# Hybrid encoder, border of mixer and feed-forward: the transposes of x's second half follow the gate's first two products in the program

## The chip, the cores and the metric

The kernel runs on one core of one Trainium2 chip. The metric is the device time of one execution in microseconds. Before the change three runs took 617.32, 617.40 and 617.11 us, a median of 617.32.

A core has five engines that work beside each other, each through its own list of instructions in order: TensorE (PE in the profile, with its weight loads as PEld), VectorE (DVE), ScalarE (ACT), GpSimd (POOL) and SyncE (SP, which issues DMAs here).

## The reference, cut to what matters

An encoder of two layers works on x of 256 tokens by 1024 columns. In each layer a mixer (three kinds of attention heads side by side) adds its output to x, and a feed-forward with a gated, convolved hidden width of 2816 does the same:

```python
for l in range(DEPTH):                       # DEPTH = 2
    x = mixer_sublayer(x, ...)               # ends in: return x + mix @ w_out_l
    x = channel_sublayer(x, ...)

def channel_sublayer(x, n2, w_gu, cw, cb, w_dn):
    h = rms_norm(x, n2)
    g, u = jnp.split(h @ w_gu, 2, axis=-1)
    g = depthwise_conv_centred(g, cw, cb)
    return x + (jax.nn.gelu(g, approximate=False) * u) @ w_dn
```

## The kernel before, in words

**Numbers as pairs.** Every large product is made of float32 values that are split into a high part and a low part (high rounded, low the rest). ACT makes a high part, DVE the low part from it. For weights these are `wp_hi` and `wp_lo`, made from `wp_raw`, the form that DMA brings in; `split` (line 607) does it in quarters of 512 columns for a unit of the feed-forward. For x they are the two halves of the tile `act_hT`.

**The border.** x lies in SBUF as `xs` (in the profile `const_x`), 128 tokens on the partitions, two token tiles t = 0 and 1, 1024 columns. The mixer ends with output projections, six pieces in `OUT_ORDER` (line 72). The last two, group 2 into columns 0 to 511 and into columns 512 to 1023, stand at lines 1246 and 1249. Each piece makes 6 matmuls for each token tile into a PSUM tile of `psa`, and then DVE adds the result to that half of `xs`.

The feed-forward needs x with its columns on the partitions. `split_T` (line 649) does this for one half of x: four column blocks k, two token tiles each, so 8 transposes on PE into two PSUM tiles of the pool `psw`; then for each k ACT writes the high part with the norm's gain, and DVE the low part. Line 1248 does the first half (k = 0 to 3), between the two projections. `mean_squares` (line 673, called at 1251) lets ACT sum the squares of x for the norm's scale, in four pieces, and POOL finishes it. The scale itself, `r2`, is applied later to the products, so transposes needn't wait for it.

**Gate and up.** The feed-forward goes through 11 steps of 256 hidden columns in the order of `FFN` (line 74): G0, U0, G1, D0, U1 and so on (G gate, U up, D down). A gate or up product is `half_up` (line 1259). It has two output tiles j = 0, 1 in `psw`, and for each of them eight column blocks k. What is called a product in this text is one `part(j, k)`, two matmuls: high weights with both parts of x (512 columns) and low weights with the high part (256 columns). G0 is called with `first=True`, and has the second half's `split_T` inside (line 1274): the first half's eight products (k = 0 to 3 for j = 0 and 1), then the transposes, then k = 4 to 7, then `row_scale`, two transposes of `r2`. A down step adds to four tiles in `psa` that stay until the end.

**What orders the work.** The code doesn't issue instructions as it is read. It writes them into a `Plan`. `order` (line 303) then chooses, one by one, among all the operations whose predecessors are placed, the one that can start first by the planner's own costs and handover times; among those with equal starts the one of the lower rank goes first (lines 366 and 367):

```python
                    if at is not None and (best is None or (at, o.rank) < best[:2]):
                        best = (at, o.rank, i)
```

The start `at` is the latest of the operands' readiness, the engine's freedom, and the freedom of a buffer for a tile that is used for the first time. The rank is the place in the program plus a shift (line 260). Casts and low halves of weights have a shift of 50 (`SPLIT_LATER`, line 56), so they stand behind what comes up to 50 places later, when both could start. Buffers of one pool are given out in the order of the tiles' first use in the program (`t.turn`, line 308; line 326 holds a tile back until its turn). `psw` has four. The planned order of each engine is then what the chip does; each engine waits on semaphores for what it needs.

Weights are loaded ahead: `unit` (line 625) is called by each product and brings the split of the next unit and the loads of those behind it. So U0's weights are cast and split while G0 is computed, and G0's while the last projection is. There are four buffers of `wp_raw` and two each of `wp_hi` and `wp_lo`.

The profile gives line 413 for every instruction, the one in `emit` that hands a planned operation to its engine. So instructions are told apart by engine, operation and tiles.

Of the kernel before, what the change touches and what calls it, by code (L numbers as in the profile page):

```python
# [455 lines left out]
def encoder_kernel(  # L456
# [168 lines left out]
    def unit():  # L625

        i = taken[0]
        taken[0] += 1
        with nc.later(SPLIT_LATER):
            while len(raws) < min(i + AHEAD + RAWS - PARTS, len(views)):  # L630
                load(len(raws))
            while len(parts) < min(i + AHEAD, len(views)):
                split(len(parts))
        return parts[i]
# [14 lines left out]
    def split_T(srcs, hi, lo, k0, g, name):  # L649


        n = g.shape[1]
        for b in range(0, n, 2):
            m = min(2, n - b)
            ps = psw.tile([P, 2, S], F32, tag="w", name=f"pt_{name}_{b}")
            for i in range(m):
                k = b + i
                for t in range(NT):
                    nc.tensor.transpose(
                        ps[:, i, t * P : (t + 1) * P], srcs[t][:, k * P : (k + 1) * P], ident  # L660
                    )
            for i in range(m):
                k = b + i
                h, o = hi[:, k0 + k], lo[:, k0 + k]
                nc.scalar.activation(h, ps[:, i], AF.Copy, scale=g[:, k : k + 1])
                nc.vector.scalar_tensor_tensor(
                    o, ps[:, i], g[:, k : k + 1], h.bitcast(F32), ALU.mult, ALU.subtract
                )

    def halves(h):  # L670
        return [xs[:, t, h * 512 : (h + 1) * 512] for t in range(NT)]
# [144 lines left out]
    for l in range(DEPTH):  # L816
# [442 lines left out]
        def half_up(name, first=False):  # L1259

            wh, wl = unit()
            ps = [psw.tile([P, 2, S], F32, tag="w", name=f"{name}{j}") for j in range(2)]

            def part(j, k):
                js = slice(j * P, (j + 1) * P)
                nc.tensor.matmul(ps[j], wh[:, k, js], h2[:, k], start=k == 0, stop=False)
                nc.tensor.matmul(ps[j][:, 0], wl[:, k, js], h2_hi[:, k], start=False, stop=k == KD - 1)

            if first:
                for k in range(4):  # L1270
                    part(0, k)
                for k in range(4):
                    part(1, k)
                split_T(halves(1), h2_hi, h2_lo, 4, gains[:, 2, l, 4:8], f"n2{l}1")
                for k in range(4, KD):
                    part(0, k)
                for k in range(4, KD):
                    part(1, k)
                row_scale()
                return ps  # L1280
            for j in range(2):
                for k in range(KD):
                    part(j, k)
            return ps

        def row_scale():

            for t in range(NT):
                nc.tensor.transpose(
                    rps[:, t * P : (t + 1) * P], r2[:, t : t + 1].to_broadcast([P, P]), ident  # L1290
                )
            nc.vector.tensor_copy(rb, rps[:, :S])
# [11 lines left out]
        def gate(s):  # L1304
            nm = f"{l}_{s}"
            Gs = joined(half_up(f"G{nm}", s == 0), f"Gs{nm}")
            nc.vector.tensor_tensor(Gs, Gs, rb.unsqueeze(1).to_broadcast([P, 2, S]), op=ALU.mult)
            A = act.tile([P, 2, S], F32, tag="s2k", name=f"A{nm}", bufs=NS2K)
            for j in range(2):
                f = 2 * s + j  # L1310
                col = lambda i: cw[:, 22 * i + f : 22 * i + f + 1]
                nc.scalar.activation(A[:, j], Gs[:, j], AF.Identity, bias=col(3), scale=col(1))
                nc.vector.scalar_tensor_tensor(
                    A[:, j, 1:S], Gs[:, j, 0 : S - 1], col(0), A[:, j, 1:S], ALU.mult, ALU.add
                )
                nc.vector.scalar_tensor_tensor(
                    A[:, j, 0 : S - 1], Gs[:, j, 1:S], col(2), A[:, j, 0 : S - 1], ALU.mult, ALU.add
                )
            B = act.tile([P, 2, S], F32, tag="s2k", name=f"B{nm}", bufs=NS2K)
            nc.scalar.activation(B, A, AF.Gelu)  # L1320
            made[s] = B

        def up(s):
            nm = f"{l}_{s}"
            C = joined(half_up(f"U{nm}"), f"C{nm}")
            nc.vector.tensor_tensor(C, made[s], C, op=ALU.mult)
            ch = act.tile([P, 2, S], F32R, tag="ch", name=f"ch{nm}", bufs=2)
            cl = act.tile([P, 2, S], F32R, tag="cl", name=f"cl{nm}", bufs=2)
            nc.scalar.copy(ch, C)
            nc.vector.tensor_tensor(cl, C, ch.bitcast(F32), op=ALU.subtract)  # L1330
            ready[s] = (ch, cl)
# [114 lines left out]
```

## Time and profile before

| | |
|---|---|
| median of 3 runs | 617.32 us (617.11 to 617.40) |
| profiled execution, span from the first to the last instruction | 615.5 us |
| instructions | 9869 |
| busy PE / DVE / ACT / POOL | 98% / 79% / 70% / 14% |
| HBM traffic | 196 GB/s over the span |
| granted clock of TensorE | 1.000 |

The profiled execution's own time is known by its span alone: 615.5 us, 1.8 us under the median of the runs, which also holds what lies before the first and behind the last instruction.

Views of the trace give a start, a duration, the engine, the operation, and the tiles as output<-inputs. A row ending in x4 stands for four instructions in a row, with the time from the first's start to the last's end; since instructions of one engine overlap a little in the pipeline, rows of single instructions overlap too. In brackets stands how long the engine was idle before the row, and what ended the wait. Layer 0's border lies at about 114 to 133 us, layer 1's at 414 to 433 us.

### The profile page before, as it was taken

The numbers are of one execution on the slowest core, as the hardware profiler recorded it, in microseconds if no ns is written. First come the engines' busy times: TensorE is split into PE (matmuls) and PEld (weight loads), VectorE is DVE, ScalarE is ACT, GpSimd is POOL, SyncE is SP. The second block draws the span as 40 slices with busy tenths as digits, with TensorE's granted clock in tenths as the row PEclk, the third lists the DMA queues.
The fourth block names the chain that finished last, engine by engine and source line by source line (L and its number), as shares of the span: only waits on it lengthen the run. The fifth ranks groups of instructions, "written<-read, shape, count | busy, mean of one in ns | idle before, by whom it ended". The sixth has DMA issues, their size and how long they took to land.

```text
span 615.5 us, 9869 instructions
## 1 busy us (share of the span) xinstructions
PE 604.9 (98%) x3484; PEld 523.7 (85%) x3484; DVE 486.9 (79%) x1000; ACT 428.3 (70%) x1064; POOL 84.0 (14%) x136
## 2 busy tenths in 40 slices
PE   8999999999999999999999999998999999999997
PEld 7998878888888888888899988887888888888885
DVE  4888989888778988878867797867877777777774
ACT  6888989686566677666588898866755656556651
POOL 2741230212400000000032213333000000000000
PEclk9999999999999999999999999999999999999999
DMA  8894313656596999988445644554565566555501
GB/s 287 275 291 143 102 35 104 208 192 195 164 252 235 364 353 325 309 278 269 154 150 173 222 137 171 205 175 135 179 231 171 176 204 205 166 180 201 185 21 68
DMA packets 85073, 121.44 MB, mean 197 GB/s; under 512 B 9864, under 2 KB 69608, under 8 KB 85024
## 3 DMA queue, kind: packets, MB, share of 16 engines
q1 hardware_dynamic: 82752, 112.17, 55.6%
q0 software_dynamic: 1728, 8.39, 4.0%
q8 instruction: 27, 0.44, 0.3%
q10 hardware_dynamic: 544, 0.26, 0.2%
q14 instruction: 22, 0.18, 0.1%
HBM read 110.93 MB, written 9.88 MB: 196 GB/s over the span
## 4 chain that ended last, share of the span: by engine, by line
PE 92%; DVE 3%; ACT 2%; issue 1%; DMA 1%; POOL 0%; SPq 0%; DVEq 0%; ACTq 0%
PE psw_w L413 49%; PE psa_a L413 43%; DVE const_x L413 1%; ACT act_s2k L413 1%; DVE wp_lo L413 1%; DMA wp_raw<-in_w_in_dram 1%; DVE act_hT L413 1%; ACT act_hT L413 1%; ACT wp_hi L413 1%; POOL small_rstd L413 0%; ACT act_mixT_hi L413 0%; POOL small_ms L413 0%; SPq L413 0%; DVE act_mixT_lo L413 0%; DVE small_ss L413 0%
## 5 line engine op out<-in xcount | busy, mean ns | idle before, releaser
L413 DVE TENSOR_TENSOR wp_lo<-wp_raw,wp_hi 128x512 fp32r<-128x512 f32 (+2 forms) x332 | 232.3, 731 | 42.9 <-ACT wp_hi L413 41.4
L413 PE MATMUL psw_w<-act_hT,wp_hi 128*128 128x512 f32 x704 | 247.8, 397 | 2.1 <-DVE act_hT L413 2.1
L413 ACT CAST wp_hi<-wp_raw 128x512 fp32r<-128x512 f32 (+2 forms) x332 | 203.1, 662 | 26.1 <-PE psw_w L413 15.3
L413 PE MATMUL psw_w<-act_hT,wp_lo 128*128 128x256 f32 x704 | 196.1, 279 | 0.1
L413 PEld LDWEIGHTS psw_w<-act_hT,wp_hi 128*128 128x128 f32 x704 | 131.9, 188 | 34.1 <-DVE act_hT L413 3.0
L413 PEld LDWEIGHTS psw_w<-act_hT,wp_lo 128*128 128x128 f32 x704 | 132.6, 188 | 1.5 <-DVE wp_lo L413 0.4
L413 PE MATMUL psa_a<-wp_hi,act_hT 128*128 128x384 f32 (+2 forms) x448 | 112.8, 332 | 0.7 <-ACT act_hT L413 0.5
L413 ACT COPY act_s2k<-psw_w 128x256 f32<-128x256 f32 x88 | 32.4, 373 | 76.3 <-PE psw_w L413 76.3
L413 PEld LDWEIGHTS psa_a<-wp_hi,act_hT 128*128 128x128 f32 x448 | 77.9, 189 | 3.8 <-ACT act_hT L413 1.0
L413 PE MATMUL psa_a<-wp_lo,act_hT 128*128 128x384 f32 (+2 forms) x224 | 74.7, 334 | 0.0
L413 PE MATMUL psa_a<-wp_lo,act_ch 128*128 128x512 f32 x176 | 69.5, 395 | 0.0
L413 PE MATMUL psa_a<-wp_hi,act_ch 128*128 128x512 f32 x176 | 69.4, 394 | 0.0
L413 PE MATMUL psa_a<-wp_hi,act_cl 128*128 128x512 f32 x176 | 65.8, 394 | 0.0
L413 DVE TENSOR_TENSOR act_s2k<-psw_w,act_s2k 128x256 f32<-128x256 f32 x88 | 36.8, 422 | 31.1 <-ACT act_s2k L413 30.7
L413 PEld LDWEIGHTS psa_a<-wp_lo,act_hT 128*128 128x128 f32 x224 | 42.3, 189 | 2.0 <-DVE wp_lo L413 1.0
L413 PEld LDWEIGHTS psa_a<-wp_hi,act_ch 128*128 128x128 f32 x176 | 33.1, 188 | 7.9
L413 PEld LDWEIGHTS psa_a<-wp_hi,act_cl 128*128 128x128 f32 x176 | 33.2, 188 | 7.8
L413 PEld LDWEIGHTS psa_a<-wp_lo,act_ch 128*128 128x128 f32 x176 | 33.1, 188 | 6.9
L413 DVE SCALAR_TENSOR_TENSOR act_s2k<-act_s2k,act_cw,act_s2k 128x255 f32<-128x255 f32 x88 | 36.9, 478 | 1.5 <-ACT act_s2k L413 1.3
L413 POOL TENSOR_TENSOR small_rstd<-small_ms,const_mh 128x6 f32<-128x6 f32 (+2 forms) x26 | 31.6, 1216 | 2.2
L413 ACT ACTIVATE act_s2k<-act_s2k,act_cw 128x256 f32<-128x256 f32 x44 | 24.1, 595 | 9.8 <-DVE act_s2k L413 9.4
L413 PE MATMUL psw_w<-act_ch,const_v 128*128 128x256 f32 x128 | 28.6, 286 | 1.1 <-ACT act_s2k L413 1.1
(112 smaller groups left out, 779.3 us busy)
## 6 DMA issues: line engine op xcount, KB each, us to landing
wp_raw<-in_w_gate_up_dram SPq DMA_DIRECT2D x44, 1024.0 KB, 5.1
wp_raw<-in_w_down_dram SPq DMA_DIRECT2D x22, 1024.0 KB, 4.8
wp_raw<-in_w_in_dram SPq DMA_DIRECT2D x14, 768.0 KB, 5.3
wp_raw<-in_w_in_dram SPq DMA_DIRECT2D x8, 1024.0 KB, 6.3
wp_raw<-in_w_out_dram SPq DMA_DIRECT2D x8, 768.0 KB, 6.4
dram_khi<-act_mixT_hi SPq DMA_DIRECT2D x4, 768.0 KB, 4.3
dram_klo<-act_mixT_lo SPq DMA_DIRECT2D x4, 768.0 KB, 5.6
wp_lo<-dram_klo POOLq DMA_DIRECT2D x4, 768.0 KB, 4.8
```

What stands on the lines that cost most here:

```text
L413: getattr(o.engine.real, o.method)(*map(real, o.args), **{k: real(v) for k, v in o.kw.items()})
```

## The change

In `half_up`, for G0 alone, the call that transposes and splits x's second half moves up in the program: it follows the product of k = 0 for the two output tiles, and the other six products of the first half follow it. The products of k = 1 to 3 keep their order. No instruction is added, removed or altered, in either layer; what the planner is given is another sequence, and so other ranks.

```diff
             if first:
-                for k in range(4):
-                    part(0, k)
-                for k in range(4):
-                    part(1, k)
+                for j in range(2):
+                    part(j, 0)
                 split_T(halves(1), h2_hi, h2_lo, 4, gains[:, 2, l, 4:8], f"n2{l}1")
+                for j in range(2):
+                    for k in range(1, 4):
+                        part(j, k)
                 for k in range(4, KD):
                     part(0, k)
                 for k in range(4, KD):
```

## The prediction

> **What bounds the kernel now.** I read the page first, then the busy time by stretches, then who PE waits for, then the order of time at the two borders of mixer and feed-forward.
>
> ```profile
> span 615.5 us, 9869 instructions
> ## 1 busy us (share of the span) xinstructions
> PE 604.9 (98%) x3484; PEld 523.7 (85%) x3484; DVE 486.9 (79%) x1000; ACT 428.3 (70%) x1064; POOL 84.0 (14%) x136
> ```
>
> PE is busy 98% of the span, so a change is worth what it takes out of PE's own waits, 615.5 - 604.9 = 10.6 us at first sight. In the next view each stretch has its length, then busy time of PE, PEld, DVE, ACT and POOL, then the granted clock.
>
> ```profile
> 114.00:133.00 19.00, 17.86 (x100) 14.58 (x99) 16.32 (x33) 14.69 (x34) 4.31 (x6) 1.00 0.60 197
> 133.00:304.00 171.00, 171.00 (x901) 145.67 (x901) 141.56 (x239) 111.92 (x203) 9.52 (x18) 1.00 0.80 265
> 304.00:311.50 7.50, 7.50 (x43) 6.35 (x42) 5.19 (x9) 4.57 (x14) 0.00 (x0) 1.00 0.56 165
> 311.50:414.00 102.50, 101.91 (x691) 93.17 (x690) 79.82 (x223) 85.23 (x288) 29.25 (x43) 1.00 0.53 177
> 414.00:433.00 19.00, 17.31 (x92) 13.96 (x92) 14.04 (x27) 11.43 (x29) 4.66 (x7) 1.00 0.40 131
> ```
>
> The feed-forward of layer 0 (133 to 304) holds no idle time of PE at all, layer 1's mixer (311.5 to 414) 0.59 us. The borders hold 1.14 us (114 to 133) and 1.69 us (414 to 433). The clock is 1.00 everywhere. Who ends PE's waits:
>
> ```profile
> PE psw_w L413 <- DVE act_hT L413: 2.1, 2, 1.1
> PE psw_w L413 <- ACT act_s2k L413: 1.7, 2, 1.1
> ```
>
> The largest is a wait for `act_hT`, the transposed and split x, twice: once for each layer, at the border. Now layer 0's border in order of time, engine by engine (DVE, ACT, then PE's weight loads):
>
> ```profile
> 122.22 1.65 DVE L413 SCALAR_TENSOR_TENSOR act_hT<-psw_w,const_gains,act_hT 128x256 fp32r<-128x256 f32 x4
> 123.79 0.74 DVE L413 SCALAR_TENSOR_TENSOR const_x<-psa_a,small_rstd,const_x 128x512 f32<-128x512 f32 x1
> 124.45 2.68 DVE L413 TENSOR_TENSOR wp_lo<-wp_raw,wp_hi 128x512 fp32r<-128x512 f32 x4
> 127.17 1.66 DVE L413 SCALAR_TENSOR_TENSOR act_hT<-psw_w,const_gains,act_hT 128x256 fp32r<-128x256 f32 x4
> 128.75 1.28 DVE L413 TENSOR_TENSOR wp_lo<-wp_raw,wp_hi 128x512 fp32r<-128x512 f32 x2
> ...
> 123.17 1.15 ACT L413 CAST wp_hi<-wp_raw 128x512 fp32r<-128x512 f32 x2
> 124.56 0.63 ACT L413 ACTIVATE act_s2k<-const_x 128x512 f32<-128x512 f32 x1 [0.24 <-DVE const_x L413]
> 125.10 0.19 ACT L413 ACTIVATION_READ_ACCUMULATOR act_s2k<-const_x 128x1 f32 x1
> 125.19 1.13 ACT L413 CAST wp_hi<-wp_raw 128x512 fp32r<-128x512 f32 x2
> 126.30 1.57 ACT L413 ACTIVATE act_hT<-psw_w,const_gains 128x256 fp32r<-128x256 f32 x4
> ...
> 125.55 0.92 PEld L413 LDWEIGHTS psw_w<-const_ident,const_x 128*128 128x128 f32 x8
> 127.71 0.19 PEld L413 LDWEIGHTS psw_w<-act_hT,wp_hi 128*128 128x128 f32 x1 [1.25 <-DVE act_hT L413]
> ...
> 130.62 0.38 PE L413 MATMUL psw_w<-const_ident,small_rx 128*128 128x128 f32 x2
> ```
>
> The last piece of x's second half (token tile 1) is written at 123.79 + 0.74 = 124.53. Its transposes load only from 125.55, when all eight products over the first half are through. Eight transposes take 0.92 us of loads, until 126.47. Then PE has nothing left: products 4 to 7 need the second half's high parts (ACT, 126.30) and low parts (DVE, 127.17), and the next load is at 127.71, after 1.25 us. Two things in front of those splits count. ACT is casting weights until 126.32, and DVE makes four low halves of weights (0.67 us each) from 124.45 to 127.13. Counting the eight low halves of G0's and U0's weights, the first two of these four are G0's last, the other two U0's first. Layer 1:
>
> ```profile
> 424.78 0.75 DVE L413 SCALAR_TENSOR_TENSOR const_x<-psa_a,small_rstd,const_x 128x512 f32<-128x512 f32 x1
> 425.44 3.09 DVE L413 TENSOR_TENSOR wp_lo<-wp_raw,wp_hi 128x512 fp32r<-128x512 f32 x5
> 428.53 1.66 DVE L413 SCALAR_TENSOR_TENSOR act_hT<-psw_w,const_gains,act_hT 128x256 fp32r<-128x256 f32 x4
> 430.11 0.68 DVE L413 TENSOR_TENSOR wp_lo<-wp_raw,wp_hi 128x512 fp32r<-128x512 f32 x1
> ...
> 424.99 1.13 ACT L413 CAST wp_hi<-wp_raw 128x512 fp32r<-128x512 f32 x2
> 426.02 0.63 ACT L413 ACTIVATE act_s2k<-const_x 128x512 f32<-128x512 f32 x1
> 426.55 0.18 ACT L413 ACTIVATION_READ_ACCUMULATOR act_s2k<-const_x 128x1 f32 x1
> 426.64 1.12 ACT L413 CAST wp_hi<-wp_raw 128x512 fp32r<-128x512 f32 x2
> 427.67 1.55 ACT L413 ACTIVATE act_hT<-psw_w,const_gains 128x256 fp32r<-128x256 f32 x4
> ...
> 424.91 0.19 PEld L413 LDWEIGHTS psw_w<-act_hT,wp_lo 128*128 128x128 f32 x1 [0.40 <-DVE wp_lo L413]
> 426.78 0.92 PEld L413 LDWEIGHTS psw_w<-const_ident,const_x 128*128 128x128 f32 x8
> 429.07 0.19 PEld L413 LDWEIGHTS psw_w<-act_hT,wp_hi 128*128 128x128 f32 x1 [1.37 <-DVE act_hT L413]
> ```
>
> The same picture: x is whole at 425.53, transposes load from 426.78 to 427.70, and the next product loads at 429.07, after 1.37 us. Here DVE makes five low halves (0.62 us each) first, two of G0 and three of U0. One more wait, 0.40 us at 424.91, is for the low half of weights for product 2.
>
> **The change part by part.** Nothing is added or removed: the same 16 matmuls over the first half, 8 transposes, 4 high and 4 low splits; no DMA and no queue of SP or POOL is moved past. What changes is the rank of these operations in the planner, which takes the operation that can start first and, among equals, the one of lower rank. Before, the transposes rank behind all eight products of the first half; after, behind two of them, one for each output tile (their PSUM tiles keep their turn, so those two must stand first). So PE's queue will read: two products, the four transposes of token tile 0 (that x is ready, and their PSUM buffers come free as DVE's splits of 122.22 go on), products, the four transposes of token tile 1 as soon as x is ready, and the remaining products.
>
> Step 1, PE's own time. It does the same work in another order. Without a wait it is through with both groups when it was before: its next load could be at 126.47 in layer 0. In layer 1 it is 427.70, or 427.30 if the 0.40 us wait goes too, since product 2 then comes later than its weights; I take 427.30.
>
> Step 2, the chain behind the transposes, layer 0. x is ready at 124.53, so the last transposes stand at about 124.7 instead of 125.55 and later. ACT takes x's last square at 124.56, to 125.10 + 0.19 = 125.29. Then the high split ranks before U0's casts, which moved it to 126.30 before; one takes under 0.5 us (four in 1.57), so 125.79. DVE has done G0's two low halves at 124.45 + 2 x 0.67 = 125.79. From the start of the first low split to PE's load it took 127.71 - 127.17 = 0.54 us, so the load is at 126.33. PE arrives at 126.47: no wait is left, with 0.14 us to spare. Gain 127.71 - 126.47 = 1.24 us.
>
> Step 3, the same for layer 1. x is ready at 425.53; ACT is free after x's last square at 426.73, high split by 427.23. DVE has done G0's two at 426.68; the split is not ready then, U0's first low half is, so it goes first, to 425.44 + 3 x 0.62 = 427.30. Load at 427.84, PE arrived at 427.30: 0.54 us of wait stay. Gain 429.07 - 427.84 = 1.23 us.
>
> What I don't see in the trace: how many low halves of U0 the planner leaves ahead of the split. Each costs 0.62 to 0.67 us at a border. The bounds are none in layer 1 (high split at 427.23, load at 427.77, gain 1.30) and both in layer 0 (load at 126.33 + 1.34 = 127.67, gain about 0); for layer 1 all three (load at 429.07, gain 0). Above that, if ACT takes the split before x's last square in layer 1, only DVE's 426.68 and PE's own 427.30 bind, and the gain is 1.77. I take none and one, since that is what is ready when DVE comes free. If the planner sets the last transposes before x is ready, PE stands still behind them, at worst right after tile 0's. That uses up the same spare time and no more, since products are left for afterwards: what is lost is only what goes beyond the chain's own time.
>
> Step 4, the transposes now come in two or three groups rather than one. The trace of before doesn't show what a return to products costs there; I bound it below by nothing (a gain is excluded, since no load is saved) and above by one transpose's own load, 0.92 / 8 = 0.115 us. With about four extra groups in both layers that is 0 to 0.46 us. I take 0.1: the two transposes at 130.62 stand between products, and no wait is noted there.
>
> Step 5, does the gain reach the end? Behind the border PE is the bound for 171 us without an idle moment, so time won at the front stays won if weights keep up. U0's casts and low halves now come behind the splits. DVE's sum of work is the same, and it has no idle time here, so U0's last low half is still done at 128.75 + 1.28 = 130.03. U0 then begins about 1.2 us before its old 130.62, at 129.4; it needs its first quarter at once and the last after six of its first eight products, 3/4 of the 2.9 us that eight products take (127.71 to 130.62), at 131.5. In the new order the first quarter is done at 125.79 + 1.66 + 0.67 = 128.1. This cover of over 1 us hides the shift; without it each microsecond late would be one lost.
>
> Sum: -1.24 - 1.23 + 0.1 = -2.4 us. The profiled execution has a span of 615.5 us, 1.8 under the runs' median of 617.32 (what lies around the span); I take the difference over to the median: **614.9 us**.
>
> The waits above are read from the weight loads (1.25 and 1.37), not from the matmuls, whose rows give shorter ones. The Trainium skill (Perfetto Trace Analysis, "Identifying the Most-Contended Engine") says that busy time of matmuls is no good measure of the distance to the roofline, and that the share of weight loads is. By the matmuls' waits (2.1 in the row above) the sum would be about 0.5 us smaller; the trace sides with the page, as 604.9 us busy against 523.7 of loads leaves room that the first figure hides.
>
> **The rivals.**
>
> Partly (19%): more low halves or casts stay ahead of the second half's splits. For it speaks that the planner picks by earliest start, and weights are always ready; against it, that ACT's rank order lets the split go first. One half more in each layer gives -2.4 + 0.67 + 0.62 = -1.1, 616.2 us; one more in one layer 615.5; both of U0's in layer 0 and one more in layer 1 616.8.
>
> Nothing moves (5%): if in the planner's own times x is ready only when the eight products are through, the order is the old one and the time 617.3. Against it: x is whole 1.0 us (layer 0) and 1.25 us (layer 1) before the first transpose loads.
>
> Slower by re-planning (11%): the planner writes the order of everything behind this point, and layer 1's mixer, where PE, ACT and DVE alternate closely, may come out in a worse order, since DMA arrivals don't shift along. The price is the wait of the size that PE already shows for ACT, 1.1 us the longest. It decides from three such waits on (3.3 against 2.4): four give 617.3 - 2.4 + 4.4 = 619.3 us. Against it: that mixer holds 0.59 us of idle PE in 102.5 now, and a common shift leaves the planner's comparisons as they are.
>
> Clock (1%): products of the first half and transposes now alternate; if transposes let the granted clock fall to half while G0's last eight products run (2.9 us from 127.71 to 130.62), each border would lose 2.9 us: 617.3 - 2.4 + 5.8 = 620.7. Against it: in 114 to 133 eight transposes in a row and a pause of 1.25 us left the clock at 1.00. The Trainium skill (TensorE: Matmul & The Clock Gate, "Part 4: PE-mode transpose") says that transposes don't count as busy for the gate. No run here shows a clock below 1.00 behind transposes, so this stays small.
>
> Better than forecast (3%): the re-planned order also loses waits elsewhere; under 614.3.
>
> **How the numbers follow.** The forecast has 61% and its own range is 614.3 to 615.4: the largest gain is 1.24 + 1.77 = 3.0 with no cost of regrouping, the smallest 2.47 less 0.46 of regrouping, 2.0. The range for 8 in 10 adds the partial case up to its 616.8: 614.3 to 616.8. A measurement of this kernel tells about 0.2% (1.2 us) from no change; faster means under 616.1. Faster: 61 + 3 + 12 of the partial 19 = 76%. Same: the other 7 of the partial, and nothing moves, 5 = 12%. Slower: 11 + 1 = 12%.
>
> **What would show it.** In the changed profile the transposes of `const_x` at each border stand in groups, the first within 1 us after the first product; the rows "PE psw_w <- DVE act_hT" of 2.1 us shrink to under 0.7; ACT's four `act_hT` directly follow x's last square; the stretch of the feed-forward stays without idle PE. Step 2 is wrong if DVE still shows four low halves in a row ahead of `act_hT`; step 5 if PE shows new waits for `wp_lo` at U0; step 4 if loads pause after each group. The forecast fails if layer 1's mixer gains idle time of PE.

## The result and the profile after

| | runs | median us | ratio to before, 95% |
|---|---|---|---|
| before | 11 | 617.11 (616.42 to 618.11) | |
| changed | 11 | 615.91 (615.35 to 616.62) | 0.9978 [0.997, 0.9986] |

Of 617.11 us the interval is a gain of 0.9 to 1.9 us, about 1.4.

The forecast gain was 2.4, and 615.91 us lies outside the 614.3 to 615.4 that the prediction gave its forecast, though inside the wider 614.3 to 616.8.

The head of the changed kernel's page, then PE's waits (some rows), then four of the stretches (length; busy PE, PEld, DVE, ACT, POOL; clock):

```profile
span 614.9 us, 9864 instructions
## 1 busy us (share of the span) xinstructions
PE 605.8 (99%) x3484; PEld 523.8 (85%) x3484; DVE 487.4 (79%) x1000; ACT 428.1 (70%) x1064; POOL 82.5 (13%) x136
```
```profile
PE psw_w L413 <- ACT act_s2k L413: 1.7, 2, 1.1
...
PE psw_w L413 <- DVE const_x L413: 0.9, 2, 0.5
...
PE psw_w L413 <- DVE act_hT L413: 0.4, 1, 0.4
```

In the kernel before, PE's wait for x was:

```profile
PE psw_w L413 <- DVE const_x L413: 0.5, 1, 0.5
```

The changed kernel's stretches:

```profile
114.00:133.00 19.00, 18.48 (x103) 15.00 (x102) 16.85 (x34) 14.59 (x34) 3.98 (x6) 1.00 0.55 184
133.00:304.00 171.00, 171.00 (x900) 145.50 (x899) 141.76 (x239) 111.58 (x203) 10.12 (x18) 1.00 0.81 266
311.50:414.00 102.50, 101.93 (x693) 93.23 (x692) 80.06 (x223) 85.47 (x289) 28.94 (x43) 1.00 0.52 176
414.00:433.00 19.00, 18.13 (x98) 14.67 (x97) 14.63 (x28) 12.09 (x30) 3.69 (x8) 1.00 0.38 126
```

The five instructions less in the head (9864 for 9869) are semaphore instructions; every engine's counted work is the same. PE's waits for `act_hT` went from 2.1 us to 0.4, while those for `const_x` (x itself) rose from 0.5 to 0.9. The borders hold 0.52 and 0.87 us of idle PE, where there were 1.14 and 1.69. The feed-forward of layer 0 still has none, layer 1's mixer 0.57 us as before (0.59), the clock is 1.00. So the new order works where it was put, and not fully. Layer 0's border, engine by engine (DVE, ACT, PE's weight loads, PE's matmuls):

```profile
125.03 2.08 DVE L413 TENSOR_TENSOR wp_lo<-wp_raw,wp_hi 128x512 fp32r<-128x512 f32 x3
127.15 1.66 DVE L413 SCALAR_TENSOR_TENSOR act_hT<-psw_w,const_gains,act_hT 128x256 fp32r<-128x256 f32 x4
...
125.15 0.63 ACT L413 ACTIVATE act_s2k<-const_x 128x512 f32<-128x512 f32 x1 [0.23 <-DVE const_x L413]
...
125.78 0.60 ACT L413 CAST wp_hi<-wp_raw 128x512 fp32r<-128x512 f32 x1
126.29 1.55 ACT L413 ACTIVATE act_hT<-psw_w,const_gains 128x256 fp32r<-128x256 f32 x4
...
123.34 0.19 PEld L413 LDWEIGHTS psw_w<-act_hT,wp_hi 128*128 128x128 f32 x1 [0.38 <-DVE act_hT L413]
...
124.03 0.14 PEld L413 LDWEIGHTS psw_w<-const_ident,const_x 128*128 128x128 f32 x1
...
124.62 0.14 PEld L413 LDWEIGHTS psw_w<-const_ident,const_x 128*128 128x128 f32 x1
...
125.43 0.79 PEld L413 LDWEIGHTS psw_w<-const_ident,const_x 128*128 128x128 f32 x6
...
127.69 0.19 PEld L413 LDWEIGHTS psw_w<-act_hT,wp_hi 128*128 128x128 f32 x1 [0.72 <-DVE act_hT L413]
...
125.65 0.82 PE L413 MATMUL psw_w<-const_ident,const_x 128*128 128x128 f32 x6
...
127.69 0.50 PE L413 MATMUL psw_w<-act_hT,wp_hi 128*128 128x512 f32 x1 [0.40 <-DVE act_hT L413]
```

One transpose of token tile 0 for each PSUM tile stands between products, and six transposes follow together from 125.43. Only one of U0's low halves is left ahead of `act_hT` on DVE (three `wp_lo`, two of them G0's), and one cast on ACT. Still a wait of 0.72 us stays. In layer 1:

```profile
424.45 0.68 DVE L413 TENSOR_TENSOR wp_lo<-wp_raw,wp_hi 128x512 fp32r<-128x512 f32 x1
425.05 0.74 DVE L413 SCALAR_TENSOR_TENSOR const_x<-psa_a,small_rstd,const_x 128x512 f32<-128x512 f32 x1
425.71 1.89 DVE L413 TENSOR_TENSOR wp_lo<-wp_raw,wp_hi 128x512 fp32r<-128x512 f32 x3
427.75 1.66 DVE L413 SCALAR_TENSOR_TENSOR act_hT<-psw_w,const_gains,act_hT 128x256 fp32r<-128x256 f32 x4 [0.16 <-ACT act_hT L413]
...
425.25 1.12 ACT L413 CAST wp_hi<-wp_raw 128x512 fp32r<-128x512 f32 x2
426.28 0.63 ACT L413 ACTIVATE act_s2k<-const_x 128x512 f32<-128x512 f32 x1
...
426.91 1.54 ACT L413 ACTIVATE act_hT<-psw_w,const_gains 128x256 fp32r<-128x256 f32 x4
...
425.85 0.64 PEld L413 LDWEIGHTS psw_w<-const_ident,const_x 128*128 128x128 f32 x6 [0.71 <-DVE const_x L413]
...
428.75 0.19 PEld L413 LDWEIGHTS psw_w<-act_hT,wp_hi 128*128 128x128 f32 x1 [0.16 <-issue]
```

Here PE now stands before the six transposes for 0.71 us of loads, because x's last update is done at 425.05 + 0.74 = 425.79, and the other five of the first half's eight products, which could have run, are behind them in its queue. In exchange the wait for `act_hT` is gone.

For all kernels below a border is measured in the same way: **G0's sixteen products**, from the start of the first to the start of U0's first, in the rows of PE's matmuls. This holds the eight transposes of x and the two of `r2`. Each figure is from one profile. Between two profiles of one program layer 0's border differs by 0.02 us at most, layer 1's by up to 0.21, so a smaller difference in layer 1 tells nothing.

| kernel | layer 0 us | layer 1 us | sum against before |
|---|---|---|---|
| before (second profile) | 8.01 (7.99) | 8.37 (8.32) | |
| changed (second profile) | 7.39 (7.40) | 7.42 (7.21) | -1.57 (-1.70) |
| new order in layer 0 alone | 7.40 | 8.24 | -0.74 |
| new order in layer 1 alone | 7.99 | 7.40 | -0.99 |
| changed, U0 behind | 7.30 | 7.17 | -1.91 |
| before, U0 behind | 8.00 | 8.23 | -0.15 |
| changed, one block a tile | 7.41 | 7.64 | -1.33 |
| before, one block a tile, U0 behind | 7.80 | 7.93 | -0.65 |
| changed, x first | 7.41 | 7.19 | -1.78 |
| changed, all three | 7.12 | 6.75 | -2.51 |
| changed, U0 behind and x first | 7.30 | 6.69 | -2.39 |

For the changed kernel -1.57 and -1.70 lie within the 0.9 to 1.9 us that the times show.

### The profile page after: what moved, and what is told of

Same layout as the page of the kernel before. It is cut to its first block, busy times and chain, and to the rows that moved or that the text cites. A ratio compares the mean times of both kernels' runs of the same rounds, so it can differ in the third digit from the quotient of the medians.

```text
span 614.9 us, 9864 instructions
## 1 busy us (share of the span) xinstructions
PE 605.8 (99%) x3484; PEld 523.8 (85%) x3484; DVE 487.4 (79%) x1000; ACT 428.1 (70%) x1064; POOL 82.5 (13%) x136
## 2 busy tenths in 40 slices
DMA packets 85073, 121.44 MB, mean 198 GB/s; under 512 B 9864, under 2 KB 69608, under 8 KB 85024
## 4 chain that ended last, share of the span: by engine, by line
PE 93%; DVE 2%; ACT 2%; issue 1%; DMA 1%; POOL 0%; SPq 0%; DVEq 0%; ACTq 0%
PE psw_w L413 50%; PE psa_a L413 43%; DVE const_x L413 1%; ACT act_s2k L413 1%; DMA wp_raw<-in_w_in_dram 1%; DVE act_hT L413 1%; ACT act_hT L413 1%; ACT wp_hi L413 0%; DVE wp_lo L413 0%; POOL small_rstd L413 0%; ACT act_mixT_hi L413 0%; POOL small_ms L413 0%; SPq L413 0%; DVE act_mixT_lo L413 0%; DVE small_ss L413 0%
```

## The experiments

**1 and 2. One layer at a time.** An `if l == 0` (or `l == 1`) around the new order, the old one in the other layer.

> The new order in layer 0 alone, the old one in layer 1. My theory: the two borders act apart and a gain at a border stays to the end. Then the stretch from G0's first product to the transposes of the scale takes 7.26 us in layer 0 (7.87 before) and 8.24 in layer 1 as before, and the time is 0.6 us under before's. Rival: the rest of the program gives some of it back (between the two borders the profile of the change was 0.3 us longer than before's); then the stretches are the same but the time is only 0.2 to 0.3 us under before's.

> The new order in layer 1 alone. My theory: 7.87 us at layer 0's border as before, 7.28 at layer 1's (8.24 before), time 1.0 us under before's; together with the run of layer 0 alone the two add to what the whole change gave (1.2 to 1.6). Rival: layer 1's gain needs the shift from layer 0, or its order comes out otherwise; then the stretch is nearer to 8.24 and the time within 0.4 us of before's.

Layer 0 alone took 616.95 us, ratio 0.9993 [0.9984, 1.0002], layer 1 alone 616.41, 0.9982 [0.9973, 0.9991]. From G0's first product to the transposes of `r2` they have 7.26 and 8.11 us, and 7.86 and 7.26; in the kernel before these are 7.87 and 8.24. So the two gains, 0.61 and 0.98, are separate, and each is the changed kernel's at that border. From layer 0's transposes of `r2` to layer 1's G0 the first took 293.53 us, 0.40 more than the 293.13 before, the second 293.04; runs 9 and 10 show where such a difference comes from. The times agree with the borders within their intervals; layer 0 alone can't be told from no change by its time, so its gain is read from the profile.

**3 and 4. U0 out of the way.** `unit` no longer splits U0 while G0 is called; this is done behind the second half's `split_T`, and may not be placed before ACT's last high split. Once on the changed kernel, once on the old order.

```diff
-            wh, wl = unit()
+            wh, wl = unit(wait=first)
...
                 split_T(halves(1), h2_hi, h2_lo, 4, gains[:, 2, l, 4:8], f"n2{l}1")
+                with nc.not_before("ACT"):
+                    split_ahead()
```

> The change, and the splitting of U0's weights is put behind ACT's last high split of x's second half, so no cast and no low half of U0 stands in front. My theory: the shortfall in layer 0 is U0's one cast and one low half that stayed ahead (0.60 to 0.67 us); layer 0's stretch falls from 7.26 to about 6.65 us and nothing waits for act_hT there; layer 1's stays within 0.15 of 7.28, since there DVE waited for ACT and PE for x. Time 0.5 to 0.6 us under the change's, 1.7 to 1.8 under before's. Rival: PE's transposes come too late for more; the stretch in layer 0 stays above 7.1 and the time within 0.2 us of the change's.

> The old order of products and transposes, with U0's splitting put behind as in the run of the change with it. It tells how much of the old gap was U0's work in the way and how much the late transposes. My theory: each had its part. Without U0's work the high split starts when the transposes are through: layer 0's first product over the second half loads about 0.7 us earlier than before (7.87 to about 7.2 us), layer 1's about 0.8 (8.24 to about 7.4), time about 1.5 us under before's, no worse than the change itself. Rival: the late transposes alone make the gap; then the stretches fall by under 0.3 us each and the time stays within 0.5 us of before's.

The changed kernel so altered took 615.23 us, 0.9967 [0.9954, 0.9979]; the old order 617.18, 0.9996 [0.9987, 1.0005]. To the transposes of `r2` the first has 7.17 and 7.03 us, the second 7.87 and 8.10. The old order is the one that tells, and there the rival held and not the theory. Its layer 0 (DVE, ACT, loads, PE):

```profile
124.48 1.28 DVE L413 TENSOR_TENSOR wp_lo<-wp_raw,wp_hi 128x512 fp32r<-128x512 f32 x2
127.20 1.66 DVE L413 SCALAR_TENSOR_TENSOR act_hT<-psw_w,const_gains,act_hT 128x256 fp32r<-128x256 f32 x4 [1.44 <-ACT act_hT L413]
...
126.33 1.57 ACT L413 ACTIVATE act_hT<-psw_w,const_gains 128x256 fp32r<-128x256 f32 x4 [1.02 <-PE psw_w L413]
...
125.58 0.91 PEld L413 LDWEIGHTS psw_w<-const_ident,const_x 128*128 128x128 f32 x8
127.74 0.19 PEld L413 LDWEIGHTS psw_w<-act_hT,wp_hi 128*128 128x128 f32 x1 [1.25 <-DVE act_hT L413]
...
125.70 1.03 PE L413 MATMUL psw_w<-const_ident,const_x 128*128 128x128 f32 x8
```

U0's casts and low halves are gone from ahead of `act_hT`, ACT idles 1.02 us and DVE 1.44 us, and PE waits the same 1.25 us as before. So U0's work, which the prediction named as what stands in front of the splits, held up nothing in layer 0; in layer 1 the wait fell from 1.37 to 1.25 us. What PE waited for is a **chain behind the transposes**: 125.70 (the first transpose on PE) to 126.33 (first high split) 0.63 us, to 127.20 (first low split) 0.87, to 127.74 (product's load) 0.54, together 2.04. In the changed kernel it is the same chain, from 125.65 on PE over 126.29 and 127.15 to 127.69: 2.04 again. In the first link the high split of a column block is held until all four transposes of its PSUM tile are through: the program's `footprint` (line 132) counts every use of a PSUM tile as a use of its whole bank, so the planner takes the four for what the split needs. In the second the first low split starts when both high splits of that tile are through. The planner asks there for the block's own high split alone; what adds the other was not followed, and runs 5 and 6 show only that it goes with the shared tile.

On the new order, U0's removal gave layer 0 only 0.09 us (7.39 to 7.30; its chain is 125.14 to 127.08, 1.94). Layer 1 has 0.25 less than the first profile of the changed kernel and 0.04 less than its second, which settles nothing. The time is 0.7 us under the changed kernel's, more than the borders give; layer 1's feed-forward behind G1's first product took 172.83 us in this profile and 173.27 in the changed kernel's (see runs 9 and 10). ACT's square of x's last piece, which stands ahead of the high splits, starts at 425.27 here, as soon as x is ready (425.17), and no longer behind two casts (425.25 to 426.28 above). What keeps PE is now x itself: its loads wait 0.70 us for `const_x`.

**5 and 6. One column block in each PSUM tile.** This takes away what makes the chain's first two links long. On the changed kernel, and on the old order with U0 behind:

```diff
-        for b in range(0, n, 2):
-            m = min(2, n - b)
-            ps = psw.tile([P, 2, S], F32, tag="w", name=f"pt_{name}_{b}")
+        m = 1 if k0 == 4 and name[:2] == "n2" else 2
+        for b in range(0, n, m):
+            ps = psw.tile([P, m, S], F32, tag="w", name=f"pt_{name}_{b}")
```

> The changed kernel, but the second half's transposes go into four PSUM tiles of one column block each instead of two tiles of two blocks. Theory (the gap is a chain behind the last transposes' first tile: 0.63 us to ACT's high split, 0.87 to DVE's first low, 0.54 to the product's load, 2.04 us in the changed kernel, and its first two links are long because a tile of two blocks is handed on as a whole): the chain shrinks to about 1.4 us, layer 0's stretch from G0's first product to the transposes of r2 goes from 7.26 to about 6.7 us, layer 1's from 7.28 to about 7.0 (there PE's wait for x stays), time about 0.8 us under the changed kernel's. Rival (U0's casts and low halves ahead of the splits, or the wait for a free PSUM buffer, bind as soon as the chain is shorter): layer 0 at 7.1 us or above, time within 0.3 us of the changed kernel's.

> The kernel before, with U0's casts and low halves behind the second half's high splits (as in the fourth run) and with one column block in each PSUM tile. Theory (chain by tiles): the wait before product 4, 1.25 us in the fourth run, falls to about 0.6 us in both layers, the stretches from 7.87 and 8.10 to about 7.25 and 7.5 us, although the transposes stand where they stood. Rival (only the place of the transposes counts): 7.8 and 8.0 us, wait 1.2 us.

The changed kernel so altered, layer 0 (DVE, ACT, loads, PE):

```profile
125.82 0.87 DVE L413 SCALAR_TENSOR_TENSOR act_hT<-psw_w,const_gains,act_hT 128x256 fp32r<-128x256 f32 x2 [0.16 <-ACT act_hT L413]
...
125.31 0.84 ACT L413 ACTIVATE act_hT<-psw_w,const_gains 128x256 fp32r<-128x256 f32 x2
...
124.79 0.36 PEld L413 LDWEIGHTS psw_w<-const_ident,const_x 128*128 128x128 f32 x2
...
126.36 0.21 PEld L413 LDWEIGHTS psw_w<-const_ident,const_x 128*128 128x128 f32 x2 [0.47 <-DVE act_hT L413]
...
128.50 0.13 PEld L413 LDWEIGHTS psw_w<-const_ident,small_rx 128*128 128x128 f32 x1 [0.40 <-issue]
...
125.01 0.38 PE L413 MATMUL psw_w<-const_ident,const_x 128*128 128x128 f32 x2
```

The chain is as short as the theory had it: first transpose of the group on PE at 125.01, high split 125.31 (0.30), low 125.82 (0.51), PE released at 126.36 (0.54), 1.35 us in place of 2.04. But what PE is released for is the third PSUM tile's transposes: `psw` has four buffers, G0's outputs hold two, so blocks 6 and 7 wait until DVE has read blocks 4 and 5. Then comes another pause of 0.40 us, before the first transpose of `r2`, which the planner has set ahead of G0's last products here. So the border did not get shorter (7.41 against 7.39, and 7.64 in layer 1): on the border's length the rival was right, on the chain the theory. Since a transpose of `r2` moved, the expected 6.7 us to that mark can't be read; the sixteen products are the fair measure. The time, 615.32 us, 0.9967 [0.9954, 0.9979], is lower than these borders explain by about 0.7 us. The interval reaches a gain of 1.3, which they do explain; and from G1's first product to the last down product this profile has 172.70 and 172.93 us in the two layers, 0.64 less together than the kernel before (173.01 and 173.26).

The old order with one block: chain 125.57 to 127.03, 1.46 us (2.04 in the fourth run), wait 1.10 for 1.25, border 7.80 and 7.93 for 8.00 and 8.23. Of the chain's 0.58 us less, 0.20 reach the border, for the same reason: blocks 6 and 7 stand behind it. To the transposes of `r2` it has 7.67 and 7.79 us: under the rival's 7.8 and 8.0 and well above the theory's 7.25 and 7.5. The time is 617.10 us, 0.9998 [0.9989, 1.0007]: the 0.65 us won at the borders don't show in it, and behind each border stands a new wait of 0.4 us, which the eighth run has too.

**7. x ahead of G0's weights, layer 1.** The changed kernel, with three of G0's four low halves placed behind x's last update on DVE.

```diff
+            if c and i in held:
+                held[i].append((low, c, e))
+            else:
+                low(c, e)
...
         for _ in out_projections(OUT_ORDER[5:]):
             pass
+        if l == 1:
+            with nc.later(SPLIT_LATER), nc.not_before("DVE"):
+                for low, c, e in held[len(views) - len(FFN)]:
+                    low(c, e)
```

> The changed kernel, with the last three quarters of the low halves of G0's weights in layer 1 put behind the last update of x on DVE. Theory (in layer 1 the transposes wait at the head of PE's queue for x, 0.4 to 0.7 us, because DVE makes a low half of G0 ahead of x's last update): that wait goes, layer 1's stretch falls from 7.28 to about 6.9 us, layer 0's stays at 7.26, time 0.3 to 0.4 us under the changed kernel's. Rival (the chain behind x binds, and G0's low halves are then late for PE): a wait for the low halves of weights appears before products 2 to 4, the stretch is 7.2 us or more.

616.11 us, 0.9976 [0.9967, 0.9984]. PE's loads and ACT at layer 1's border:

```profile
424.62 0.72 PEld L413 LDWEIGHTS psw_w<-const_ident,const_x 128*128 128x128 f32 x6
...
427.65 0.19 PEld L413 LDWEIGHTS psw_w<-act_hT,wp_hi 128*128 128x128 f32 x1 [0.54 <-DVE act_hT L413]
...
424.61 1.12 ACT L413 CAST wp_hi<-wp_raw 128x512 fp32r<-128x512 f32 x2
425.64 0.63 ACT L413 ACTIVATE act_s2k<-const_x 128x512 f32<-128x512 f32 x1
```

The wait for x is gone, and a wait of 0.54 us for `act_hT` stands in its place: the transposes load 1.0 us after G0's first product starts (423.61), but ACT still casts U0's weights for 1.0 us before it takes the last square. The border is 7.19 us, 0.23 less than in the first profile of the changed kernel and the same as in its second (7.21). To the transposes of `r2` it is 7.05 us, between the theory's 6.9 and the rival's 7.2, and the time is not under the changed kernel's. The rival's wait for low halves of weights did not come, but its first half held, that the chain behind x binds: one wait was exchanged for the next.

**8. All three.**

> The changed kernel with all three: U0's casts and low halves behind the second half's high splits, one column block in each PSUM tile, and layer 1's low halves of G0 behind x's last update. Theory: PE then has work at both borders almost without a break, sixteen products of 0.345 us, eight transposes of 0.11 us and little else, 6.6 to 6.7 us in both layers, against 7.26 and 7.28 in the changed kernel: 1.2 us under it, 2.4 us under the kernel before, with up to 0.4 us either way from the pace of the feed-forward. Rival (U0's weights, made later, now hold PE at U0's first product, or G0's do in layer 1): a wait of 0.4 us or more for the low halves of weights behind the border, total no better than the third run's, 615.2 us.

615.29 us, 0.9968 [0.9956, 0.9981]. The borders are 7.12 and 6.75 us. In layer 1 no wait for `act_hT` is left and one of 0.21 us for x. From 423.17 to the transposes of `r2` at 429.78 it is 6.61 us there, as expected; layer 0 has 6.98, since PE waits 0.47 us for a buffer for the third PSUM tile. Of the 2.5 us less at the borders part is given back in a new wait behind each, 0.39 us before the first down product:

```profile
141.18 0.19 PEld L413 LDWEIGHTS psa_a<-wp_hi,act_ch 128*128 128x128 f32 x1 [0.39 <-ACT act_ch L413]
```

It stands in layer 1 too (441.35, 0.39 us), and in the sixth run (0.40 and 0.39), in none of the third. So the rival's size of wait and its total were right, at another place: not weights are late, but the gated hidden values that ACT makes for D0. Both runs with this wait have one block a tile and U0 behind; how the two together delay ACT was not followed further. The theory's 6.6 to 6.7 us came in layer 1 alone.

**11. Both without the smaller tiles.** U0 behind and x first, as in runs 3 and 7, with two blocks a tile.

> The changed kernel with U0's casts and low halves behind the second half's high splits and layer 1's low halves of G0 behind x's last update, but with two column blocks in each PSUM tile as before. Theory (in layer 1 the chain, ACT's casts ahead of the square, and x's last update bind one behind the other; each alone exchanges one wait for another, both together leave the chain): G0's sixteen products take 7.3 us in layer 0 as in the third run, and 6.75 to 6.9 in layer 1, where the third run had 7.17 and the seventh 7.19; D0's first product does not wait for its input as it does by 0.39 us in the eighth run, so the time is 0.2 to 0.4 us under the third run's, about 615.0 us. Rival (layer 1 needs the shorter chain of one block in each tile): 7.1 us or more in layer 1, time 615.2 us or above.

614.35 us, 0.9951 [0.9937, 0.9965]: the lowest median, and its interval lies below the changed kernel's, though it overlaps those of runs 3, 5 and 8. Layer 1's border (DVE, ACT, loads):

```profile
423.11 1.40 DVE L413 SCALAR_TENSOR_TENSOR const_x<-psa_a,small_rstd,const_x 128x512 f32<-128x512 f32 x2
...
424.61 0.63 ACT L413 ACTIVATE act_s2k<-const_x 128x512 f32<-128x512 f32 x1
...
425.24 1.55 ACT L413 ACTIVATE act_hT<-psw_w,const_gains 128x256 fp32r<-128x256 f32 x4
...
424.56 0.65 PEld L413 LDWEIGHTS psw_w<-const_ident,const_x 128*128 128x128 f32 x6
```

x is whole at 424.51, the transposes load at 424.56, the square starts at 424.61, the high splits at 425.24, and PE's rows show no wait at all: 6.69 us, less than the theory's lowest (6.75). Where the six transposes start on PE 1.15 us behind G0's first product (424.63 - 423.48), the chain of 2 us fits beside the products, and the smaller tiles are not needed. Behind G1's first product layer 1's feed-forward took 172.83 us here, 0.43 less than before, and layer 0's 173.36, 0.35 more, so the two nearly cancel. Layer 0 has 7.30 us and its wait of 0.61, as in the third run. So in layer 1 the two limits are shown, ACT's casts in front of the square and x's last update behind a low half of G0: either alone gives at most 0.25 us, both together 0.73 (7.42 to 6.69), or 0.52 against the second profile. In layer 0 the place of the transposes and the chain bind; why the planner leaves them behind products there, x being ready, was not tried.

**9 and 10. The same two kernels again.** In the changed kernel's first profile layer 0's feed-forward behind G0 and U0 took 0.34 us more than before, without idle PE. From a gate or up block's start to the next with a down step between, it takes there mostly 11.11 or 11.23 us, and without one 5.55 or 5.64, in turns, and in this profile more of the slow ones fell into the last steps.

> The kernel before, unaltered, profiled a second time. Question: within the feed-forward PE computes a pair of gate and up blocks in 11.11 or in 11.23 us without any wait, and layer 0's feed-forward is 0.34 us longer in the changed kernel for that reason. Theory (the pace is a matter of the single execution): the pattern of paces differs from the first profile's, by some tenths of a microsecond in all. Rival (it belongs to the kernel's instructions): the same pattern, layer 0's feed-forward again 173.0 us behind G0 and U0.

> The changed kernel, unaltered, profiled a second time. Theory (the pace is a matter of the single execution): another pattern of 11.11 and 11.23 us, layer 0's feed-forward behind G0 and U0 between 172.7 and 173.4 us. Rival (it belongs to the kernel): the same pattern and 173.35 us again. Both: the borders come out at 7.26 and 7.28 us again, since these follow from the order of instructions.

PE's rows of the changed kernel for G1's first product and the last down product, first profile, then second:

```profile
136.47 0.40 PE L413 MATMUL psw_w<-act_hT,wp_hi 128*128 128x512 f32 x1
...
309.82 0.39 PE L413 MATMUL psa_a<-wp_hi,act_cl 128*128 128x512 f32 x1
```
```profile
135.63 0.40 PE L413 MATMUL psw_w<-act_hT,wp_hi 128*128 128x512 f32 x1
...
308.64 0.40 PE L413 MATMUL psa_a<-wp_hi,act_cl 128*128 128x512 f32 x1
```

173.35 and 173.01 us for the same program, as the tenth run's theory had it; the kernel before had 173.01 and the same pattern both times, as the ninth run's rival had it. So in layer 0 the pace can differ between executions of one program, and the 0.34 us needn't be the change's. In layer 1 all four of these profiles have 173.26 or 173.27 us, and those of runs 3, 7 and 11 have 172.83; there nothing tells whether the execution or the program makes the difference. The tenth run's other expectation held in layer 0 (7.26 us to the transposes of `r2`) and not in layer 1 (7.08, not 7.28): x came 0.2 us sooner there, and PE's loads waited 0.51 us for it instead of 0.71. (The first profile also began G0 0.84 us later than the second, 123.34 against 122.50.) The second changed profile took 615.51 us, the first 616.62. What sets the pace was not found.

## Why the prediction was right in sign and too large

**Right:** the direction, the place, and that the time stays won. That 615.91 us lies in the wide range is in part luck: that range took in the case of more low halves and casts ahead of the splits, and what kept the gain from the forecast's 2.4 us was something else. What the trace was to show came, but for a cast between x's last square and `act_hT` in layer 0: groups of transposes, the first 0.7 us after the first product (123.34 to 124.03 by loads), the row of 2.1 us down to 0.4, no idle PE in the feed-forward, no new wait for `wp_lo` at U0. The sign named for step 2 being wrong, four low halves in a row ahead of `act_hT`, did not show (there are three), and step 2 was wrong all the same: the sign watched another cause.

**Step 1** held in layer 0: measured from G0's first product, PE would have been ready for product 4 at 127.69 - 0.72 - 123.34 = 3.63 us, against the predicted 126.47 - 122.75 = 3.72.

**Step 2** is the one that failed: "one takes under 0.5 us, so 125.79" and "the load is at 126.33". It took the split of one block as one high and one low split, each starting as soon as its engine was free, and took the transposes at 124.7 for done. Shifted by 0.59 us, the difference of the two starts of G0, the changed trace has the first of the six on PE at 125.06, the high split at 125.70 and not 125.29, the low at 126.56 and not 125.79, the load at 127.10 and not 126.33. So the load is 0.77 us later than predicted: 0.36 us, since the planner left the six transposes behind products although x was ready at 124.53 (124.38 + 0.74 = 125.12 before the shift); 0.05 more to the high split, and 0.36 from high to low. The trace of the kernel before had the evidence, in PE's rows beside those that the prediction shows:

```profile
125.66 1.03 PE L413 MATMUL psw_w<-const_ident,const_x 128*128 128x128 f32 x8
127.71 0.50 PE L413 MATMUL psw_w<-act_hT,wp_hi 128*128 128x512 f32 x1 [1.01 <-DVE act_hT L413]
```

125.66 on PE to 126.30, 127.17 and 127.71 is the same chain, 2.05 us. The prediction took ACT's casts until 126.32 and DVE's low halves until 127.13 for the cause, because they ended at the right moment. The fourth run took them away and the chain stayed. With a fixed chain layer 0's gain is simply how much earlier the transposes start: 125.66 - 122.75 = 2.91 us behind G0's first product before, 125.65 - 123.34 = 2.31 after, 0.60 us; measured 0.61 to the transposes of `r2`.

**Step 3** was off by less: predicted 1.23, measured 0.96 in that mark (8.24 to 7.28), 1.10 between the second profiles (8.18 and 7.08). x was ready as said (425.79 less the shift of 0.28 is 425.51, predicted 425.53), and ACT's square came behind the casts as said. The low split started 0.17 us later than the 427.30 predicted (427.75 less 0.28), again for the link from high to low: 426.91 to 427.75 is 0.84 us, where "high split by 427.23" took 0.5. The bound "the planner sets the last transposes before x is ready" came true in layer 1 and cost what was said, the spare time and no more: PE waited 0.71 us there and not at all for `act_hT`.

**The four transposes of tile 0 in a row** did not come. Within one PSUM tile they go in the program's order, block by block with both token tiles, since the planner counts the tile as a whole (`footprint`), so only one in each could go ahead of x's second tile.

**Step 4** was right near its lower bound. A lone transpose among the products shifts what follows by 0.11 us (from 124.03 to 124.49 on PE 0.46 us pass, 0.35 without one), and six in a row take 0.11 each: a return to products costs nothing that can be seen. The 0.1 us was not spent.

**Step 5** held: U0 shows no wait. **The loads' waits**, which the prediction took for the size of the gain, were not the better figure: in layer 0 they fell from 1.25 to 0.72, by 0.53 us, and the matmuls' own from 1.01 to 0.40, by 0.61, which is what the border gained.

**The rivals.** Partly, with 19%, comes nearest by the result: in layer 0 one low half and one cast of U0 did stay ahead, where none was taken, and its 615.5 us for that case is close. But by the third and fourth runs its mechanism isn't the cause. Re-planning: outside the two borders the order of every engine's instructions is the same as before (semaphore instructions aside), so there was nothing to lose. The clock stayed at 1.00. Two of the prediction's small sums are 0.1 us off: 617.3 less 2.0 is 615.3 and not 615.4, and the last partial case comes to 616.9 and not 616.8. Neither changes what is said here.

## What to carry to other kernels

When an engine waits at the end of a chain through PE, ACT and DVE, add up the chain's links from an earlier execution before blaming the work that stands in front of them: work that ends just when the link starts may only have filled the time. A tile that is handed on as a whole makes the first reader wait for the last writer, and cutting it finer helps only as far as there are buffers for the pieces. Of several limits that lie within half a microsecond of each other, removing one shows the next.

## What was not expected of the hardware

Two profiles of one program differ by 0.34 us in a feed-forward of 173 us in which PE never idles: the pace of a block and a down step changes between 11.11 and 11.23 us, with no wait in the records, and it isn't the granted clock, which is 1.00 in that stretch of both. So a single profile of this kernel can't place a gain of 0.3 us, except at a stretch that has its own waits.
